# A product-key expert layer routed by column group for four token blocks at once, with sixteen best-entry tiles summed early

## The chip, the cores and the metric

The kernel runs on one core of one Trainium2 chip. The metric is the device time of one execution in microseconds; lower is better. Times from the profile count from the start of its span.

## The reference

One decoder block on 1024 tokens of width 1024: normalisation and modulation by a conditioning vector, a projection to 14 groups of 512 columns, a gated linear attention branch and a spatial gating branch, an output projection, and then a mixer with 16384 experts of one neuron each. Only the mixer is touched here. Cut to what matters:

```python
q = einsum('btd,dq->btq', h, w_q).reshape(B, T, H, 2, 128)      # H = 8 heads
s1, s2 = einsum(q[..., 0, :], keys1), einsum(q[..., 1, :], keys2) # 128 scores each
v1, i1 = top_k(s1, 16);  v2, i2 = top_k(s2, 16)
cand = v1[..., :, None] + v2[..., None, :]                        # 256 candidates
top_s, pos = top_k(cand, 16);  idx = i1 * 128 + i2 at pos
g = softmax(top_s)
y = sum over heads and 16 entries of g * gelu(h . down[idx]) * up[idx]
x = x + gate2 * y;  out = rms_norm(x, final_norm_w)
```

## The kernel before

The 1024 tokens are eight blocks of 128, in two halves of four blocks (0 to 3, 4 to 7). Each half runs through dense stages: the 14 projection groups (`group`, L1045, eight k-steps each), the output projection (`w_out_part`), the block's rows for the mixer (`h2_part`), and the query projection in four column groups of two heads each (`w_q`, L1350). A weight tile `wt` is split into two float32r parts, `wh` on ACT and `wl` on POOL or DVE (L1036, L1038), and three matmuls stand for one product (`mm3`). After every k-step `step()` advances four queues of generators by rates of their own: `qa` (conditioning rows), `qr` (routing), `qp` (the stream of expert tiles) and `qdir` (best entries of the first half). The framework then orders the instructions of each engine; in that order each engine works them off.

`s_part` (L1390) scores one column group of one block against the keys and ranks it with `tops`: the best 8 of 128 for two heads and both key halves. When all four column groups are done, `rank` (L1383) adds for each of the four blocks a `routing` (L278): 20 candidate sums per head (`cand`, L289), the best 8 of them, gates, and the decoding of their expert numbers. Of each head the best entry stays apart (`dix`, its expert; `dgt`, its gate). The other seven entries with a gate that counts go into one list per block: `pack_list` (L252) counts them (L261), gives each a place, splits the list (`th`, `tl`) and writes it to DRAM. A head of a token whose eighth gate still counts is rare: `rare` (L324) collects such heads of a group of blocks, fetches their scores (`qsc`, L362) and ranks 16 of them. The groups are blocks 0 to 3, 4 and 5, 6 and 7.

The experts' rows are worked in tiles of 128. Each tile is one gather of 128 rows of 8 KB (`uv`, L440: down and up row together) on POOL's queue, a product with the token rows on DVE, gelu and scaling on ACT, and a sum into PSUM on PE (`acc`, L513). A best-entry tile (`direct_list`, `direct_dot`, L450, L454) has one row per token, for one head of one block. A list tile (`entry_list`, `entry_dot`) reads 128 list places (`tps`, L462), spreads the token rows by matmuls (`hps`, L492, L493) and multiplies them with the gathered rows (L494). In the dense stage a list tile's sum is four float32r matmuls (`split_add`, L523, L524). A block has 8 best-entry tiles, 10 list tiles and one tile that adds the stored rows of its rare heads (`rare_rows`); then `finish` (L552) writes its output. Best entries of blocks 0 to 3 are summed apart in the dense stage (`direct_rows`) and added in `finish` through a stored row (L559).

`peer_stream` (L644) writes that order out by hand in `todo`: 6 rare tiles of group 0, blocks 0 to 3, and then for each of the two later groups:

```python
b = GROUPS[gi][0]
todo += [(b, j) for j in range(PH)] + [(NBLK + gi, PH + j) for j in range(NTR[gi])]
todo += [(b + 1, j) for j in range(PH)] + [(c, j) for c in (b, b + 1) for j in range(PH, last + 1)]
```

Here j below 8 is a best entry, up to 17 a list tile, 18 the rare rows; `NBLK + gi` stands for a group's rare tiles. `fill` (L701) starts the gathers ahead (2 tiles in the dense stage, 7 after) and holds back block 4 and what follows until the last query columns are ranked, the rest until the dense stage ends. After that, tiles have nine buffers in three pools (L1421).

## Time and profile before

| | us |
|---|---|
| runs, median of 3 | 1657.19 (1652.46 to 1660.2) |
| the profiled execution | 1650.64 |
| its span | 1648.5 |
| PE busy | 1440.4 (87%) |
| DVE busy | 1069.7 (65%) |
| POOL busy | 816.3 (50%) |
| ACT busy | 775.4 (47%) |

The span is one execution as the profiler saw it; the device time of the same execution lies 2.1 us around it. PE is TensorE, DVE VectorE, ACT ScalarE, POOL GpSimd, PEld the weight loads of TensorE. A busy share over the span is a mean over stages with different limits, so the stretches are read one by one: what an engine did in each, and what ended its waits. PEclk is the granted clock of TensorE as a share of full speed, and the DMA share is the mean busy share of the 16 DMA engines.

### The profile page before, as it was taken

To read this page: it belongs to the slowest core of one execution; us is meant where nothing else is said; L and a number is where in the kernel's file an instruction comes from. 1 tells how busy PE (TensorE), PEld (TensorE's weight loads), DVE (VectorE), ACT (ScalarE), POOL (GpSimd) and SP (SyncE) were. 2 spreads that over 40 slices of the span, in tenths; PEclk is the share of its full clock that TensorE was granted. 3 is DMA by queue.
4 is the path that set the end of the run, shared out by engine and by line. 5 is a ranking of instruction groups with operands and counts; after the bars stand their busy time and mean duration, and the time that the engine had idled before them with its cause. 6 is when DMAs were issued, how large, how long until landed. Compare 5 with 4: busy or idle time off the path is not lost. (4 is left out here: it accounts for less than half of the span.)

```text
span 1648.5 us, 20446 instructions
## 1 busy us (share of the span) xinstructions
PE 1440.4 (87%) x6113; PEld 1077.6 (65%) x6113; DVE 1069.7 (65%) x2906; ACT 775.4 (47%) x1708; POOL 816.3 (50%) x685
## 2 busy tenths in 40 slices
PE   4999989999998998888879999989879964898895
PEld 3777757888768886677657776867578842454442
DVE  6774653111454469978977777789895567678663
ACT  3553323333445355735445565566544443445442
POOL 4331247533374338755666677557775423323420
PEclk7999999999999999999999999999989976899997
DMA  9642533224376338757745787958866453998992
GB/s 306 230 165 85 188 117 109 94 79 141 109 244 247 116 116 301 247 159 243 265 163 188 249 305 275 343 213 283 304 214 210 168 233 115 365 417 310 409 403 96
DMA packets 124441, 363.81 MB, mean 221 GB/s; under 512 B 17577, under 2 KB 28073, under 8 KB 108194
## 3 DMA queue, kind: packets, MB, share of 16 engines
q0 software_dynamic: 30816, 178.14, 28.6%
q1 hardware_dynamic: 70272, 132.15, 24.1%
q10 hardware_dynamic: 23234, 52.14, 8.8%
q8 instruction: 49, 0.80, 0.2%
q14 instruction: 70, 0.57, 0.1%
HBM read 336.44 MB, written 25.94 MB: 220 GB/s over the span
## 5 line engine op out<-in xcount | busy, mean ns | idle before, releaser
L1038 POOL TENSOR_TENSOR wl<-wt,wh 128x512 fp32r<-128x512 f32 x257 | 360.6, 1409 | 368.5 <-ACT wh L1036 344.4
L1036 ACT ACTIVATE wh<-wt 128x512 fp32r<-128x512 f32 x368 | 228.0, 627 | 314.0 <-PE mm L173 177.3
L172 PE MATMUL mm<-wl,hTh 128*128 128x512 f32 x896 | 364.7, 407 | 9.7 <-POOL wl L1038 8.3
L171 PE MATMUL mm<-wh,hTh 128*128 128x512 f32 x896 | 336.4, 411 | 27.8 <-DVE sg L1239 8.8
L173 PE MATMUL mm<-wh,hTl 128*128 128x512 f32 x896 | 358.5, 403 | 1.4 <-DVE hTl L995 1.4
L171 PEld LDWEIGHTS mm<-wh,hTh 128*128 128x128 f32 x896 | 171.7, 193 | 78.1 <-DVE sg L1239 9.6
L172 PEld LDWEIGHTS mm<-wl,hTh 128*128 128x128 f32 x896 | 172.6, 193 | 59.4 <-POOL wl L1038 14.6
L1038 DVE TENSOR_TENSOR wl<-wt,wh 128x512 fp32r<-128x512 f32 x111 | 100.3, 905 | 165.8 <-ACT wh L1036 160.3
L173 PEld LDWEIGHTS mm<-wh,hTl 128*128 128x128 f32 x896 | 172.3, 192 | 41.8 <-DVE hTl L995 1.5
L171 PE MATMUL mm<-hTh,wh 128*128 128x512 f32 (+1 forms) x448 | 168.5, 378 | 10.9 <-ACT hTh L167 4.6
L440 POOL DMA_INDIRECT uv<-in_tab_dram,ix x94 | 102.0, 1085 | 147.2 <-PE hps L493 27.5
L172 PE MATMUL mm<-hTl,wh 128*128 128x512 f32 (+1 forms) x448 | 165.7, 371 | 1.0 <-DVE hTl L168 1.0
L173 PE MATMUL mm<-hTh,wl 128*128 128x512 f32 (+1 forms) x448 | 158.2, 373 | 6.6 <-POOL wl L1038 5.9
L494 DVE SCALAR_TENSOR_TENSOR uv<-uv,hps 128x512 f32<-128x512 f32 x148 | 98.3, 682 | 49.8 <-PE hps L493 26.1
L171 PEld LDWEIGHTS mm<-hTh,wh 128*128 128x128 f32 x448 | 87.7, 196 | 27.7 <-ACT vt L1083 5.9
L522 DVE SCALAR_TENSOR_TENSOR vl<-uv,r,vh 128x512 fp32r<-128x512 f32 x92 | 81.6, 915 | 36.4 <-ACT vh L521 33.7
L173 PEld LDWEIGHTS mm<-hTh,wl 128*128 128x128 f32 x448 | 86.5, 196 | 21.8 <-POOL wl L1038 6.8
L513 PE MATMUL acc<-uv,W 128*128 128x512 f32 x192 | 96.6, 628 | 3.5 <-ACT W L506 3.2
L172 PEld LDWEIGHTS mm<-hTl,wh 128*128 128x128 f32 x448 | 87.7, 196 | 14.5 <-DVE hTl L168 1.7
L492 PE MATMUL hps<-hh,E 128*128 128x512 f32 x148 | 76.3, 519 | 22.3 <-DVE uv L494 10.9
L513 PE MATMUL acc<-uv,Wd 128*128 128x512 f32 x128 | 63.4, 647 | 8.8 <-ACT Wd L454 6.9
L521 ACT ACTIVATE vh<-uv,r 128x512 fp32r<-128x512 f32 x92 | 62.2, 714 | 3.8 <-PE acc L523 1.4
(955 smaller groups left out, 2642.8 us busy)
## 6 DMA issues: line engine op xcount, KB each, us to landing
wt<-in_w_inp_dram SPq DMA_DIRECT2D x224, 256.0 KB
wt<-in_w_qp_dram SPq DMA_DIRECT2D x80, 256.0 KB
wada<-in_w_ada_dram SPq DMA_DIRECT2D x32, 512.0 KB
wt<-in_w_outp_dram SPq DMA_DIRECT2D x64, 256.0 KB
wada<-in_w_ada_dram SPq DMA_DIRECT2D x32, 256.0 KB
s_d<-so ACTq DMA_DIRECT2D x32, 256.0 KB
xr<-in_x_dram ACTq DMA_DIRECT2D x8, 512.0 KB
x_d<-x ACTq DMA_DIRECT2D x8, 512.0 KB
```

The source lines that it names most:

```text
L171: nc.tensor.matmul(ps, lh, rh, start=first, stop=False)
L172: nc.tensor.matmul(ps, lh, rl, start=False, stop=False)
L173: return nc.tensor.matmul(ps, ll, rh, start=False, stop=last).ins
L440: nc.gpsimd.indirect_dma_start(out=uv[:], out_offset=None, in_=tab, in_offset=bass.IndirectOffsetOnAxis(ap=ix, axis=0))
L492: nc.tensor.matmul(hps, Ej, hh[:, sl], start=True, stop=False)
L494: nc.vector.scalar_tensor_tensor(uv[:, sl], uv[:, sl], 1.0, hps, op0=OP.mult, op1=OP.mult, accum_out=r[:, 2 + n:3 + n])
L513: nc.tensor.matmul(acc[:, sl], W, v[:, sl], start=first, stop=last)
L521: nc.scalar.activation(vh, v, AF.Identity, scale=r[:, 5:6])
L522: nc.vector.scalar_tensor_tensor(vl, v, r[:, 5:6], vh.bitcast(F32), op0=OP.mult, op1=OP.subtract)
L1036: nc.scalar.activation(wh, wt, AF.Identity)
L1038: eng.tensor_tensor(wl, wt, wh.bitcast(F32), op=OP.subtract)
```

## The change

It routes by column group. `tops` now ranks into tables that hold one column group (two heads) of four blocks; right after a column group's scores `rank(q)` adds a `route` for it, so that the first three of four run beside the next columns' projection. The work of one `route` is as wide as that of one `routing` was: two heads of four blocks in place of eight heads of one. One `pack_half` then packs the lists of four blocks together, and one `rare` covers blocks 4 to 7, with 6 tiles in place of 4 and 4. In `todo`, after block 3, come the best-entry tiles of blocks 5 (four), 6 (four) and 7 (eight); their sums are stored by `rows_keep` and added in `finish`. Then come block 4's eight best entries, three of its list tiles, the six rare tiles, the rest of block 4, and blocks 5, 6 and 7 with what is left. `fill` lets a best-entry tile go in the dense stage as soon as its column group is ranked. Block rows have two buffers after the dense stage, and two rates change.

```diff
-GROUPS = ((0, 1, 2, 3), (4, 5), (6, 7))
+GROUPS = ((0, 1, 2, 3), (4, 5, 6, 7))
-NTR = (6, 4, 4)
+NTR = (6, 6)
-DA = 8
+EARLY = ((5, 4), (6, 4), (7, 8))
-RP3 = .5
+RP3 = .65
-RR = 0.5
+RR = 1.0
...
+    def pack_half(hf, tsel, rps):
+        n, b0 = NCS, hf * BH
+        bs = slice(b0, b0 + BH)
+        g, rk = tsel[:, :, 2 * n:3 * n], tsel[:, :, 0:n]
+        wk = rp.tile([P, 2, BH, n], F32, name="wk", tag="so", bufs=2)
+        nz, inc = wk[:, 0], wk[:, 1]
+        nc.vector.tensor_scalar(nz, g, TINY, None, op0=OP.is_ge)
+        nc.vector.tensor_tensor_scan(inc.rearrange("p b n -> p (b n)"), ones[:, 0:1].to_broadcast([P, BH * n]),
+                                     nz.rearrange("p b n -> p (b n)"), 0.0, op0=OP.mult, op1=OP.add)
+        nc.vector.tensor_copy(e4[:, 1:], inc[:, :, n - 1])
+        nc.vector.tensor_tensor(cnt[:, bs], e4[:, 1:], e4[:, :BH], op=OP.subtract)
+        yield
+        pst = rps.tile([P, BH], F32, name="aux", tag="aux")
+        nc.tensor.matmul(pst, ltri, cnt[:, bs], start=True, stop=True)
+        yield
...
+        nc.scalar.activation(th, tsel, AF.Identity)
+        nc.gpsimd.tensor_tensor(tl, tsel[:, :, n:3 * n], th[:, :, n:3 * n].bitcast(F32), op=OP.subtract)
+        nc.scalar.dma_start(tsh_d[hf][:, :, :3 * n + 2], th.bitcast(F32))
+        nc.scalar.dma_start(tsh_d[hf][:, :, 3 * n + 2:], tl.bitcast(F32))
+        routed.update(range(b0, b0 + BH))
...
+    def rows_keep(b, acc):
+        y = rowp.tile([P, D], F32, name="yd", tag="row")
+        nc.scalar.activation(y, acc, AF.Identity)
+        nc.scalar.dma_start(y_d[b], y)
+        summed.add(b)
...
+        seg(NBLK, range(PH, PH + NTR[0]))
+        for b in range(BH):
+            seg(b, range(0 if b not in summed else PH, last + 1))
+        for b, n in EARLY:
+            seg(b, range(n))
+        done = dict(EARLY)
+        seg(BH, range(last - AH), False)
+        seg(NBLK + 1, range(PH, PH + NTR[1]))
+        todo.extend((BH, j) for j in range(last - AH, last + 1))
+        closes[BH, last] = True
+        for b in range(BH + 1, NBLK):
+            seg(b, range(done.get(b, 0), last + 1))
...
-                if len(use) == 1 and b >= BH and b != NBLK and (b > BH or j >= DA or b not in topped):
+                if len(use) == 1 and b >= BH and b != NBLK and (j >= PH or (1, j // 2) not in topped):
                     break
...
+            elif lst and j < last:
+                rows_keep(b, accs[b])
...
-            for b in blks:
-                rank(b)
...
+                if half != 0:
+                    rank(q)
...
+            def rank(q):
+                tv, ti = tvi[q]
+                nc.vector.scalar_tensor_tensor(dixq[hf][q].rearrange("p b h -> p (b h)"), ti[:, :, 0, 0], float(NK),
+                                               ti[:, :, 1, 0], op0=OP.mult, op1=OP.add)
+                topped.add((hf, q))
+                qr.add(route(hf, q, tsel, tv, ti))
+                if q == 3:
+                    qr.add(pack_half(hf, tsel, aux))
+                    qr.add(rare(hf, aux))
...
-    use.append(peer_pools("1", "left", UVB, 1, 2, AH, EB, True))
+    use.append(peer_pools("1", "left", UVB, 2, 2, AH, EB, True))
```

How the order moves, at three places. First PE, at the second half's last scores (the four matmuls on `keyst`), before; `acc_12153` is block 4's sum, and the matmuls on `cnt` are packings and the rare count:

```order
L1394 MATMUL aux_12023<-keyst_95,qt_11964 128x128
L1394 MATMUL aux_12023<-keyst_95,qt_11966 128x128
L1394 MATMUL aux_12023<-keyst_95,qt_11968 128x128
L1394 MATMUL aux_12023<-keyst_95,qt_11970 128x128
L261 MATMUL aux_12169<-cnt_130,ltri_63 128x1
L513 MATMUL acc_12153<-uv_12074,Wd_12146 128x512 x2
L513 MATMUL acc_12153<-uv_12077,Wd_12151 128x512 x2
L513 MATMUL acc_12153<-uv_12080,Wd_12415 128x512 x2
L513 MATMUL acc_12153<-uv_12083,Wd_12441 128x512 x2
L513 MATMUL acc_12153<-uv_12086,Wd_12487 128x512 x2
```

Now; `acc_12111` is block 7's sum of best entries:

```order
L1462 MATMUL aux_12264<-keyst_95,qt_12206 128x128
L1462 MATMUL aux_12264<-keyst_95,qt_12208 128x128
L1462 MATMUL aux_12264<-keyst_95,qt_12210 128x128
L1462 MATMUL aux_12264<-keyst_95,qt_12212 128x128
L556 MATMUL acc_12111<-uv_12073,Wd_12109 128x512 x2
L556 MATMUL acc_12111<-uv_12104,Wd_12156 128x512 x2
L556 MATMUL acc_12111<-uv_12151,Wd_12202 128x512 x2
L556 MATMUL acc_12111<-uv_12197,Wd_12335 128x512 x2
L556 MATMUL acc_12111<-uv_12313,Wd_12368 128x512 x2
L556 MATMUL acc_12111<-uv_12316,Wd_12400 128x512 x2
L297 MATMUL aux_12440<-cnt_127,ltri_63 128x4
```

Eight of block 7's tiles follow the last scores, where one block's packing and block 4's tiles did; one packing with four columns stands for four.

Second PE, inside the last column group's projection, now (`mm` are the projection's sums, `acc_11825` block 6's best entries; before, no such sum stands there):

```order
L179 MATMUL mm_11951<-hTh_181,wh_12116 128x512
L180 MATMUL mm_11951<-hTl_182,wh_12116 128x512
L556 MATMUL acc_11825<-uv_11741,Wd_11792 128x512 x2
L181 MATMUL mm_11951<-hTh_181,wl_12117 128x512
L179 MATMUL mm_11952<-hTh_181,wh_12116 128x512
L180 MATMUL mm_11952<-hTl_182,wh_12116 128x512
L181 MATMUL mm_11952<-hTh_181,wl_12117 128x512
```

A best-entry sum stands between two matmuls of one product; blocks 5 and 6 have eight of them ahead of the last scores.

Third POOL, from the splitting of a list (`tl`) to the first rare gathers (`ix` from a list row, `dix` best entries), before:

```order
L273 TENSOR_TENSOR tl_12179<-tsel_12097,th_12178 128x112
L273 TENSOR_TENSOR tl_12253<-tsel_12184,th_12252 128x112
L289 TENSOR_TENSOR cidx_12447<-tif_12448 128x8x8
L289 TENSOR_TENSOR cidx_12447<-tif_12448 128x8x4 x3
L362 DMA qsc_12289<-s_d1_110,qix_12283 128x256
L418 DMA h2l_12377<-h2_d1_107,rtok1_137 128x1024
L289 TENSOR_TENSOR cidx_12746<-tif_12747 128x8x8
L289 TENSOR_TENSOR cidx_12746<-tif_12747 128x8x4 x3
L273 TENSOR_TENSOR tlq_12372<-qtsel_12347,thq_12371 128x32
L440 DMA uv_12407<-in_tab_dram,ix_12405 128x2048
L440 DMA uv_12429<-in_tab_dram,ix_12427 128x2048
```

Now:

```order
L311 TENSOR_TENSOR tl_12465<-tsel_9770,th_12464 128x448
L483 DMA uv_12498<-in_tab_dram,ix_12496 128x2048
L483 DMA uv_12537<-in_tab_dram,ix_12535 128x2048
L483 DMA uv_12581<-in_tab_dram,ix_12579 128x2048
L405 DMA qsc_12569<-s_d1_109,qix_12561 128x256
L461 DMA h2l_12679<-h2_d1_107,rtok1_133 128x1024
L279 TENSOR_TENSOR tlq_12674<-qtsel_12649,thq_12673 128x32
L483 DMA uv_12709<-in_tab_dram,ix_12707 128x2048
L483 DMA uv_12731<-in_tab_dram,ix_12729 128x2048
```

Before, the fetch of rare scores (`qsc`) stood between two routings and ahead of every list gather; now it stands behind three gathers of block 4's list, and no routing is left there.

## Rows read from the trace of the kernel before

**Rows 1.** Busy us (instructions) of PE, PEld, DVE, ACT, POOL; PEclk, DMA share, GB/s.

```profile
1240.00:1329.00 89.00, 89.00 (x438) 74.16 (x438) 42.52 (x189) 40.26 (x80) 42.66 (x34) 1.00 0.49 171
1329.00:1405.00 76.00, 35.34 (x106) 20.58 (x105) 60.69 (x395) 34.68 (x98) 25.94 (x39) 0.67 0.55 210
1405.00:1629.00 224.00, 200.74 (x574) 103.46 (x572) 152.06 (x587) 103.00 (x335) 69.92 (x70) 0.96 0.89 358
640.00:720.00 80.00, 64.74 (x230) 48.00 (x230) 75.77 (x207) 50.83 (x91) 57.48 (x49) 0.87 0.67 224
880.00:1240.00 360.00, 324.03 (x1469) 257.08 (x1468) 290.64 (x567) 206.87 (x472) 236.79 (x192) 0.95 0.75 266
```

**Rows 2.** The same view, one stretch of 40 us in the tail.

```profile
1560.00:1600.00 40.00, 36.38 (x113) 19.22 (x111) 24.65 (x99) 16.58 (x54) 14.42 (x15) 1.00 1.01 419
```

**Rows 3.** Waits of PE from 1331 to 1425 us: total, times, longest.

```profile
PE aux L261 <- ACT rd L452: 15.1, 1, 15.1
...
PE aux L261 <- DVE cnt L258: 11.3, 1, 11.3
```

**Rows 4.** Timeline of POOL: start us, us, instruction, idle before and its releaser.

```profile
1295.85 2.40 POOL L560 TENSOR_TENSOR fin<-fin,g2row 128x1024 f32<-128x1024 f32 x1 [8.16 <-DVE fin L559]
...
1336.16 1.02 POOL L440 DMA_INDIRECT uv<-in_tab_dram,dix  x1 [0.16 <-DVE ts L295]
...
1351.63 0.42 POOL L273 TENSOR_TENSOR tl<-tsel,th 128x112 fp32r<-128x112 f32 x1 [3.67 <-ACT th L272]
...
1369.97 0.98 POOL L362 DMA_INDIRECT qsc<-s_d,qix  x1 [1.87 <-DVE rtok L357]
...
1390.92 0.95 POOL L440 DMA_INDIRECT uv<-in_tab_dram,ix  x1 [5.32 <-PE tps L462]
...
1460.69 0.95 POOL L362 DMA_INDIRECT qsc<-s_d,qix  x1 [0.30 <-DVE jk L468]
...
1612.90 0.94 POOL L440 DMA_INDIRECT uv<-in_tab_dram,ix  x1 [7.49 <-PE hps L493]
```

**Rows 5.** Chain that ended last, from 1200 us on: start us, us, what.

```profile
1329.25 1.57 PE aux L1394 x14
...
1373.54 0.48 DVE qtv L190 x2
...
1388.74 0.62 PE tps L462 x2
...
1405.39 3.53 PE acc L513 x4
...
1426.42 10.57 PE acc L513 x24
...
1476.25 0.53 DVE qti L191 x3
...
1524.26 10.73 DMA uv<-in_tab_dram,ix
...
1604.19 0.23 PE hps L492
...
1610.41 1.72 PE acc L513 x4
...
1613.06 1.72 PE acc L513 x4
```

**Rows 6.** Waits of PE from 600 to 760 us.

```profile
PE mm L173 <- POOL wl L1038: 5.9, 3, 3.8
...
PE aux L261 <- DVE cnt L258: 1.8, 1, 1.8
```

**Rows 7.** Groups of DVE, 640 to 720 us, then 1331 to 1410: busy us, mean ns.

```profile
L289 DVE TENSOR_TENSOR cand<-tv 128x32 f32<-128x32 f32 (+1 forms) x8 | 5.1, 683 | 0.0
...
L450 DVE SCALAR_TENSOR_TENSOR uv<-uv,h2l 128x1024 f32<-128x1024 f32 x9 | 11.2, 1240 | 0.4 <-DMA uv<-in_tab_dram,dix 0.4
...
L289 DVE TENSOR_TENSOR cand<-tv 128x32 f32<-128x32 f32 (+1 forms) x16 | 2.2, 193 | 0.0
```

More of the change, by code (lines that the diff above doesn't have):

```diff
@@ L146, in block_kernel @@
     yr_d = [dram.tile([P, D], F32, name=f"yr_d{g}") for g in range(NG)]
-    y_d = dram.tile([BH, P, D], F32, name="y_d")
+    y_d = [dram.tile([P, D], F32, name=f"y_d{b}") for b in range(NBLK)]
     ncs_of = [NCS] * NBLK + [TOPK] * NG
-    ts_d = [dram.tile([P, 5 * n + 2], F32, name=f"ts_d{i}") for i, n in enumerate(ncs_of)]
+    tsh_d = [dram.tile([P, BH, 5 * NCS + 2], F32, name=f"tsh_d{i}") for i in range(NHALF)]
+    ts_d = [tsh_d[b // BH][:, b % BH] for b in range(NBLK)]
+    ts_d += [dram.tile([P, 5 * TOPK + 2], F32, name=f"ts_d{g}") for g in range(NG)]
     rt = ctx.enter_context(tc.tile_pool(name="rt", bufs=1))
@@ L157, in block_kernel, with dcol @@
     rcol = [rt.tile([P, len(bs)], F32, name=f"rcol{g}") for g, bs in enumerate(GROUPS)]
-    dix = [rt.tile([P, PH], I32, name=f"dix{b}") for b in range(NBLK)]
-    dgt = [rt.tile([P, PH], F32, name=f"dgt{b}") for b in range(NBLK)]
+    dixq = [[rt.tile([P, BH, 2], I32, name=f"dix{hf}_{q}") for q in range(4)] for hf in range(NHALF)]
+    dgtq = [[rt.tile([P, BH, 2], F32, name=f"dgt{hf}_{q}") for q in range(4)] for hf in range(NHALF)]
+    e4 = rt.tile([P, BH + 1], F32, name="e4")
+    nc.vector.memset(e4, 0.0)
+    def dcol(tabs, b, h):
+        return tabs[b // BH][h // 2][:, b % BH, h % 2:h % 2 + 1]
     def rstd_of(dst, ss, n, eng=nc.vector):
@@ L276, in pack_list @@
         routed.add(col)
-    def routing(b, tv, ti, rps):
-        gi, bi = GRP[b]
-        K1 = KS - 1
-        tsel = r2.tile([P, 3 * NCS + 2], F32, name="tsel")
-        cand = r2.tile([P, PH, NCAND], F32, name="cand")
-        cidx = r2.tile([P, PH, NCAND], F32, name="cidx")
-        tif = r2.tile([P, PH, 2, KS], F32, name="tif")
+    def pack_half(hf, tsel, rps):
[13 more added lines that the diff above has]
+        yield
+        off = r2.tile([P, BH], F32, name="off")
+        nc.vector.tensor_copy(start[:, bs], pst)
+        nc.vector.tensor_tensor(off, start[:, bs], e4[:, :BH], op=OP.subtract)
+        nc.vector.tensor_tensor(end[:, bs], start[:, bs], cnt[:, bs], op=OP.add)
+        rki = rp.tile([P, BH, n], I32, name="rki", tag="bits")
+        for i in range(BH):
+            nc.vector.tensor_scalar(rki[:, i], inc[:, i], off[:, i:i + 1], None, op0=OP.add)
+        nc.vector.tensor_scalar(rki, rki, P - 1, None, op0=OP.bitwise_and)
+        nc.vector.scalar_tensor_tensor(rk, rki, 1.0, nz, op0=OP.add, op1=OP.mult)
+        th = rp.tile([P, BH, 3 * n + 2], F32R, name="th", tag="v")
+        tl = rp.tile([P, BH, 2 * n], F32R, name="tl", tag="so", bufs=2)
+        nc.scalar.activation(th, tsel, AF.Identity)
[3 more added lines that the diff above has]
+        routed.update(range(b0, b0 + BH))
+        yield
@@ L285, in routing, with route @@
+    def route(hf, q, tsel, tv, ti):
+        K1, R = KS - 1, 2 * BH
+        if q == 0:
+            for i in range(BH):
+                nc.scalar.activation(tsel[:, i, 3 * NCS:3 * NCS + 2], lane1.to_broadcast([P, 2]), AF.Identity,
+                                     bias=lane0(hf * BH + i) - 1.0)
+        cand = r2.tile([P, R, NCAND], F32, name="cand")
+        cidx = r2.tile([P, R, NCAND], F32, name="cidx")
+        tif = r2.tile([P, R, 2, KS], F32, name="tif")
         nc.scalar.activation(tif[:, :, 0], ti[:, :, 0], AF.Identity, scale=float(NK))
@@ L377, in rare @@
         yield
-        yield from pack_list(tsel, TOPK, NBLK + gi, rps, "q")
+        yield from pack_rare(tsel, TOPK, NBLK + gi, rps, "q")
         yield
@@ L445, in direct_list @@
         r = pl["pq"].tile([P, 3], F32, name="rd", bufs=pl["ahead"] + 4)
-        return pl, b, h, h2, r, gather(ul, dix[b][:, h:h + 1])
+        return pl, b, h, h2, r, gather(ul, dcol(dixq, b, h))
     def direct_dot(ent):
@@ L778, in peer_rest @@
                 nc.vector.scalar_tensor_tensor(id_, sel[:, 0], float(NK), sel[:, 1], op0=OP.mult, op1=OP.add)
-                y = pg_.tile([P, D], F32, name="gy")
+                y = pl["ph"].tile([P, D], F32, name="gy", tag="hh")
                 nc.vector.memset(y, 0.0)
```

126 lines of the change are left out of this document (59 added, 67 removed).

## The prediction

> **What bounds the kernel now.** I read the stretches by engine first, then the waits, then the chain that ended last. The stretches [rows 1] show three regimes. While the last query columns of the second half are projected (1240 to 1329) TensorE is busy 89.00 of 89.00 us: whatever is put on it there costs its own length. From 1329 to 1405 it is busy 35.34 of 76 us and the DMA engines 0.55: here the scores are ready and the lists are not. From 1405 to 1629 it is busy 200.74 of 224 us with the DMA at 0.89 and 358 GB/s: the tail of gathered tiles. In a 40 us piece of that tail the DMA share is 1.01 at 419 GB/s [rows 2]; a gather brings 128 rows of 8 KB, 1.05 MB, so at that rate one costs 2.51 us, and at the tail's mean of 358 GB/s 2.93 us.
>
> The middle regime is what the change is about. TensorE's two longest waits there stand both before a list packing's count: 15.1 us, released when a best-entry tile was scaled, and 11.3 us for the counts themselves [rows 3]. The queue of gathers [rows 4] shows it from the other side: block 4's eight best-entry gathers go out from 1336.16 on, one after the other, and the next gather goes only at 1390.92, because in this order four rare tiles come next, and they need the routing of blocks 4 and 5 and the rare chain. Of 80 gathers behind the last scores (the last goes at 1612.90) only 8 are issued in the first 60 us.
>
> **What a tile costs in the tail.** On the chain [rows 5] list tiles at the end follow each other every 2.65 us (1610.41, 1613.06), 1.72 of it the four sums; six best-entry tiles take 10.57 us (x24), 1.76 each. With 2.51 us of DMA, gather and TensorE are nearly level for a list tile, and the DMA is the longer for a best-entry tile.
>
> **The change, part by part.** The clock below starts at the last scores (1329.25, first of rows 5), S.
>
> *Tiles taken out of the tail.* Before, the first rare tile is summed at 1405.39 [rows 5], S+76, with 8 best-entry tiles done and 76 tiles to go (48 list or rare, 24 best-entry, 4 of stored rare rows). After, the orders put 19 gathered tiles ahead of the first rare one: 8 of block 7, 8 of block 4, 3 lists of block 4. Behind it stand 43 list or rare tiles, 8 best-entry, 4 stored: 5 and 16 fewer. They are cheapest by TensorE, 5 x 2.65 + 16 x 1.76 = 41.4 us; by the DMA at its full rate 21 x 2.51 = 52.7; at the tail's mean rate 21 x 2.93 = 61.5. I take **57 us**, between the last two: the DMA is the nearest bound, and the tail never held its full rate throughout. Two rare tiles fewer and one rare chain fewer are in this count; so is the second buffer for a block's rows (hb 2), which I give nothing of its own.
>
> *The dense stage.* Eight early tiles (blocks 5 and 6) stand between the last projections in TensorE's order, 8 x 1.76 = +14 us where it is full. Against that the orders put four list tiles fewer among the last five hundred projection matmuls, since the first half's routing is done sooner and the stream of tiles starts sooner; such a tile has eight matmuls of the 0.23 us that the chain shows for one (1604.19 [rows 5]), so 4 x 1.8 = -7, into 880 to 1240, where TensorE idles 36 of 360 us [rows 1]. In the first half three of four routings move from 640 to 720, where VectorE is busy 75.77 of 80 us and TensorE idles 15.3 [rows 1], to the projections before. Bounds nothing and 15; I take -5, as the waits that name the routing are small (the counts, 1.8 us in 600 to 760 [rows 6]). Sum **+2**, bounds -9 and +14. Eight more products of 1.24 us [rows 7] and three routings go on VectorE beside these projections. A routing is at most 12 us: the 60.69 us of VectorE from 1329 to 1405 [rows 1] hold four and nine products. That is at most 47 us where 46.5 of the 89 are free, and four list tiles are gone: hidden, just. If that cover went, the rival on the dense stage below applies. Seven early gathers share the DMA with the weights at a share of 0.49.
>
> *The chain to the lists.* Before, block 4's list is split at 1351.63 [rows 4], S+22.4, with three products in between. After, VectorE's order has eight products ahead of the packing's end, 5 x 1.24 = +6.2, and one packing for four blocks, on 224 columns in place of 56: +2. Split at S+31. Six more products, 7.4, stand ahead of the first list row, then 5 (an estimate: 2.2 us from a list row at 1388.74 to its gather at 1390.92 [rows 4, 5], as much again for the last product's scaling and sum): first list gather at S+43. The list's way through DRAM runs beside these products, in two writes on ACT's queue where four blocks had eight. POOL's order has three list gathers and then the fetch of the rare scores, each about 1.25 us apart: S+48. That fetch took 3.6 us with an empty queue (1369.97 to 1373.54) and up to 15.6 behind gathers (1460.69 to the ranking of these scores at 1476.25) [rows 4, 5]. Three 1.05 MB gathers are ahead of it: I take 10, S+58. From there to the first rare gather before: 1373.54 to 1390.92, 17.4, S+75; to its sum 14.5 before, beside three routings on VectorE, which are gone: 7. The first rare sum comes at S+82 against S+76: **+6**, bounds -6 and +20. What is late next is the same queue: between the last of the 19 tiles and the rare ones the DMA still idles, some 20 us.
>
> *The end.* Block 7 now adds a stored sum: its last chain goes through a POOL product of 2.40 us [rows 4] that it did not have. **+3**. Three more rows of 512 KB written and read cost 3 x 1.3 us of DMA, inside the 57.
>
> **Sum.** The profiled execution took 1650.64 us: -57 + 2 + 6 + 3 = -46, 1604.6. The median of the runs shown, 1657.19, lies 6.6 above that execution; against it the forecast is **1611 us**. Bounds of the four terms against the median: 1657 - 61.5 - 9 - 6 + 3 = 1584 and 1657 - 41.4 + 14 + 20 + 3 = 1653.
>
> **Rivals.**
>
> *More is saved.* The tail's bubbles (two waits of over 10 us for a gather, one of them 10.73 us [rows 5]) lie where blocks and rare groups change; with one group and two row buffers they go, the dense end does not move, and the rare fetch finds an empty queue: 1584. For it: one group change instead of two. Against: the six rare tiles still wait for everything.
>
> *VectorE and POOL stand in each other's way in the dense stage.* The four sums of candidates of a routing took 193 ns each in the tail and 683 ns between 640 and 720, where POOL splits weights [rows 7], and TensorE waited 5.9 us for POOL's splits in 600 to 760 [rows 6]. The change moves three routings and eight products beside POOL's splits of the last columns, all of which are on POOL there. At the loss of 640 to 720 (15.3 of 80 us) the 89 us lose 17: 1628. For: those rows. Against: 640 to 720 also had the recurrent heads, and POOL is at 42.66 of 89 us here, not at 57 of 80. The Trainium skill (SBUF — State Buffer, "SBUF: two separate sides") says that VectorE instructions with two SBUF inputs and GpSimd instructions that read SBUF take one pair of ports as an exclusive lock, the loser waiting for the whole instruction. By that rule every candidate sum and product put there would wait for a split, and a split for it; the 683 against 193 ns agree, and the rule would give this rival's time rather than mine if the splits had no slack.
>
> *The one packing comes late.* All lists now hang on the last column group, on one packing and one rare chain; if the rare scores take 15.6 us and the chain slows as it did beside routing, the first rare sum comes at S+102, 20 later than taken: 1631. For: VectorE's order puts two list products ahead of the rare ranking. Against: 19 tiles are served meanwhile.
>
> *Slower.* TensorE takes its instructions in order, and the eight early sums stand at fixed places between projections. Each waits for its gather, its product and a scaled identity; if they are late, projections wait behind them. The price is eight times that lateness. From 5.8 us each the 46 us are eaten, from 6.8 us each the kernel is slower by over 0.5%; at the 10.73 us above, 1611 + 86 = 1697. Against: in 1240 to 1329 TensorE idled not at all, although list tiles stand in the same way between the same matmuls.
>
> That the change doesn't do what it says is settled by the orders: eight early tiles do stand ahead of the last scores, and eight (block 7) only behind them, and so they are priced.
>
> **How the numbers follow.** 0.5% is about what a measurement of this kernel can tell from no change. Forecast (1596 to 1626) 0.57; more is saved 0.12; the dense stage 0.14; late packing 0.11; slower 0.06. The two middle rivals together, 1648 and more, come to about 0.05 out of theirs. Faster by over 0.5% 0.88, within 0.5% 0.05, slower 0.07. The range runs from 1580, a little past the larger saving, to 1642, past each middle rival alone.
>
> **What would show it.** Right: between the last scores and the first rare sum TensorE sums 19 tiles instead of 8 and its share there rises well above 35 of 76 us; the last scores start within 10 us of 1329; the first rare sum follows them by about 82; the last stretch is about 50 us shorter at an unchanged rate. Wrong: waits for gathers or products ahead of early sums inside the projections; POOL's splits named by TensorE's waits after 1240; a rare fetch that lands later than S+65; a last stretch that shrinks by 41 or less, TensorE being its bound.

## The result, and the profile after

| | us |
|---|---|
| after, median of 4 runs | 1636.44 (1634.42 to 1637.92) |
| before, median of 4 runs | 1658.38 (1652.46 to 1660.2) |
| ratio, with 95% interval | 0.9876 (0.9854 to 0.9898) |
| the profiled execution after, its span | 1637.25, 1635.2 |

The change saves 22 us by the medians, where 46 were forecast. The time lies inside the range, at its slow end. The kernel before had medians of 1651.7 to 1658.4 in the sessions that follow, so kernels of different sessions are compared by their ratios to it.

Three points cut the profiled execution: the last row of scores on PE, the first rare sum, the end. The timeline of PE, before and then after (start us, us, instruction, idle before and its releaser):

```profile
1331.50 2.05 PE L1394 MATMUL aux<-keyst,qt 128*128 128x128 f32 x16 [0.46 <-ACT so L1396]
```

```profile
1312.38 1.22 PE L1462 MATMUL aux<-keyst,qt 128*128 128x128 f32 x4 [6.03 <-ACT qt L1415]
...
1355.35 3.68 PE L556 MATMUL acc<-uv,Wd 128*128 128x512 f32 x4 [2.43 <-ACT yd L689]
1358.86 1.95 PE L1462 MATMUL aux<-keyst,qt 128*128 128x128 f32 x16
...
1396.24 10.57 PE L556 MATMUL acc<-uv,Wd 128*128 128x512 f32 x24 [0.84 <-ACT Wd L497]
1406.24 0.64 PE L505 MATMUL tps<-thl,E 128*128 128x170 f32 x1
```

The first rare sum stands in the chain that ended last, after (start us, us, what):

```profile
1356.87 13.38 DMA s_d<-so
...
1412.89 8.16 DMA qsc<-s_d,qix
...
1433.97 1.81 DMA thl<-ts_d
...
1449.84 3.78 PE acc L556 x4
```

Before, it stood at 1405.39 [rows 5]. So, from profiled execution to profiled execution (1650.64 to 1637.25, -13.4; these two happen to lie nearer each other than the medians):

| stretch | before | after | difference | forecast |
|---|---|---|---|---|
| to the last row of scores | 1331.5 | 1358.9 | +27.4 | +2 |
| from there to the first rare sum | 73.9 | 91.0 | +17.1 | +6 |
| from there to the end of the execution | 245.2 | 187.4 | -57.8 | -57 + 3 |

The tail gave what was forecast. The expected gain was given back ahead of it, most of it before the last scores. A second execution of the changed kernel (after_again, below) has its last row of scores at 1353.8, +22.3: it reached the last columns 5 us earlier, so about 5 of the 27.4 differ from execution to execution. The same stretches by engine, after (busy us and instructions of PE, PEld, DVE, ACT, POOL; PEclk, DMA share, GB/s), answering to [rows 1]:

```profile
1240.00:1359.00 119.00, 110.35 (x487) 84.55 (x486) 79.44 (x344) 62.01 (x131) 62.16 (x59) 0.96 0.72 249
1359.00:1450.00 91.00, 57.40 (x147) 29.30 (x145) 59.23 (x304) 38.12 (x110) 28.56 (x30) 0.74 0.66 249
1450.00:1613.00 163.00, 148.88 (x448) 81.14 (x448) 108.15 (x393) 73.42 (x240) 47.92 (x47) 0.96 0.89 359
```

The last row is the tail at an unchanged rate (DMA 0.89, 359 GB/s against 0.89, 358), 61 us shorter. In the first row PE, which had been busy 89.00 of 89.00, idles 8.65 of 119. The middle row has 18 tiles where 19 were forecast, because block 7's first sum went ahead of the last row of scores (1355.35). PE is busy 57 us instead of 35, but it is 15 us longer than the one it answers to, and the DMA share is still only 0.66.

### The profile page after: what moved, and what is told of

Read it like the earlier page. It is cut to its first block, busy times and chain, and to the rows that moved or that the text cites. A ratio compares the mean times of both kernels' runs of the same rounds, so it can differ in the third digit from the quotient of the medians.

```text
span 1635.2 us, 20174 instructions
## 1 busy us (share of the span) xinstructions
PE 1428.3 (87%) x6076; PEld 1073.5 (66%) x6076; DVE 1074.3 (66%) x2766; ACT 772.5 (47%) x1682; POOL 821.9 (50%) x677
## 4 chain that ended last, share of the span: by engine, by line
PE 40%; DVE 23%; DMA 15%; issue 9%; ACT 7%; POOL 5%; ACTq 0%; DVEq 0%; POOLq 0%; SPq 0%
PE mm L180 8%; PE mm L179 8%; PE mm L181 8%; PE acc L556 7%; DMA uv<-in_tab_dram,ix 3%; DMA wada<-in_w_ada_dram 2%; POOL wl L1098 2%; DVE wl L1098 2%; DMA uv<-in_tab_dram,dix 2%; DMA uvd<-in_down_dram,dix 2%; DVE uv L537 2%; DVE vl L565 1%; PE hps L535 1%; DVE E L634 1%; DVE uvd L670 1%
## 5 line engine op out<-in xcount | busy, mean ns | idle before, releaser
L1098 POOL TENSOR_TENSOR wl<-wt,wh 128x512 fp32r<-128x512 f32 x257 | 368.6, 1440 | 379.7 <-ACT wh L1096 342.2
L565 DVE SCALAR_TENSOR_TENSOR vl<-uv,r,vh 128x512 fp32r<-128x512 f32 x92 | 91.3, 1023 | 29.7 <-ACT vh L564 28.1
L556 PE MATMUL acc<-uv,W 128*128 128x512 f32 x184 | 91.9, 625 | 3.4 <-ACT W L549 2.1
L556 PE MATMUL acc<-uv,Wd 128*128 128x512 f32 x128 | 67.5, 668 | 22.6 <-ACT Wd L497 18.7
```

The costliest lines, as they stand in the source:

```text
L556: nc.tensor.matmul(acc[:, sl], W, v[:, sl], start=first, stop=last)
L565: nc.vector.scalar_tensor_tensor(vl, v, r[:, 5:6], vh.bitcast(F32), op0=OP.mult, op1=OP.subtract)
L1098: eng.tensor_tensor(wl, wt, wh.bitcast(F32), op=OP.subtract)
```

## Experiments

Where an experiment leaves a part of the kernel out, its output is not the kernel's; it serves only to price that part. For the dense stage one stretch serves all kernels: from the second score row of the first column group (1259.40 after) to the last row of scores (1358.86), which holds the projections of the other three groups. After, and in the kernel without early tiles (hold_all, below), it holds the same 232 recorded projection matmuls.

| kernel | ratio to before (95%) | stretch, us |
|---|---|---|
| after | 0.9876 (0.9854 to 0.9898) | 99.5 |
| after_again | 0.9869 (0.9841 to 0.9897) | 99.5 |
| hold_67 | 0.9833 (0.9782 to 0.9884) | 91.3 |
| no56 | 0.9811 (0.9762 to 0.9861) | 78.9 |
| hold_all | 0.9766 (0.9716 to 0.9815) | 73.3 |
| hold_all_again | 0.9735 (0.9710 to 0.9759) | 74.0 |
| dropsum | 0.9833 (0.9788 to 0.9878) | 93.1 |
| dropscale | 0.9861 (0.9824 to 0.9897) | 89.8 |
| dropprod | 0.9801 (0.9758 to 0.9844) | 80.1 |
| nofin3 | 0.9824 (0.9805 to 0.9843) | 94.1 |
| dropsum_nofin3 | 0.9797 (0.9771 to 0.9823) | 88.6 |
| tsel_dve | 0.9848 (0.9803 to 0.9894) | 97.3 |
| hold_tsel_dve | 0.9744 (0.9704 to 0.9783) | 72.2 |

**No early tile before the dense stage ends (hold_all).**

```diff
-                if len(use) == 1 and b >= BH and b != NBLK and (j >= PH or (1, j // 2) not in topped):
+                if len(use) == 1 and b >= BH and b != NBLK:
```

> The changed kernel, but no best-entry tile of blocks 4 to 7 may start before the dense stage has ended; the list of tiles is the same, so 24 best-entry tiles and 3 list tiles now stand between the last scores and the first rare sum. Theory (the eight to nine early sums on TensorE's in-order queue are what pushed the dense end back: 16 us of their own, 8.5 us of waits, and score copies held behind their scalings on ScalarE): the last scores start at 1330 to 1335 again instead of 1358.9, the first rare sum comes at 1420 to 1430 instead of 1449.8, and the time falls by 20 to 28 us against the changed kernel, to 1608 to 1617. Rival A (the routing beside the projections is what pushed the end back): the last scores stay past 1350 and the time is that of the changed kernel or worse. Rival B (what bounds the time up to the first rare sum is the traffic of the gathers, not the chain of packing and rare scores): the last scores go back to 1332, but eight more gathers behind them push the first rare sum out again, past 1440, and less than 10 us are saved.

Measured: last row of scores at 1326.47, first rare sum at 1420.97, median 1613.73; in the repeat, beside the changed kernel in one session, 1613.14 against 1635.57. That is 22 us faster than the changed kernel, and 2.3 to 2.7% faster than the kernel before: with those of its variants below that change nothing, it is the fastest version found. The theory holds, rivals A and B do not: the traffic is heavier behind the scores (24 best-entry and 3 list tiles, DMA share 0.80 over those 94 us), yet the first rare sum comes 29 us earlier. By stretches:

```profile
1240.00:1327.00 87.00, 84.79 (x416) 69.87 (x415) 60.40 (x302) 43.78 (x85) 49.19 (x50) 1.00 0.67 229
1327.00:1421.00 94.00, 69.64 (x178) 34.29 (x176) 72.39 (x333) 48.05 (x143) 32.88 (x34) 0.84 0.80 312
1421.00:1586.00 165.00, 151.35 (x452) 81.97 (x450) 108.02 (x396) 72.90 (x241) 50.90 (x50) 0.95 0.90 362
```

One detail matters: the edit moves products, scalings and sums behind the last scores, but not all gathers. The framework still issues nine of them on POOL's queue between 1260.72 and 1326.24, and they cost the stage nothing that can be seen: TensorE is busy 71.06 of the 73.26 us. Two of the nine go out only in the last 1.5 us of the stretch, so this is shown for seven. Behind the stage it is not shown to be free: the chain that ended last there holds a write of score copies of 8.59 us (1326.94) and a load of token rows of 8.65 us (1336.55), and no run tells whether the gathers lengthen these.

> The changed kernel once more, unaltered, beside the next one on the same chip and with five rounds: its ratio to the kernel before should lie within 0.985 to 0.990 again (0.9876 before).

> The kernel without early tiles in the dense stage once more, unaltered, beside the changed kernel on the same chip. Theory: 15 to 25 us below the changed kernel, and below the kernel before by 2.2 to 2.9%. If the gap is under 8 us, the first comparison (on two chips) misled.

Both as expected (0.9869 and 0.9735).

**A half dose, and fewer tiles behind the scores (hold_67, no56).** hold_67, and what no56 has beside hold_all's edit:

```diff
-                if len(use) == 1 and b >= BH and b != NBLK and (j >= PH or (1, j // 2) not in topped):
+                if len(use) == 1 and b >= BH and b != NBLK and (b > 5 or j >= PH or (1, j // 2) not in topped):
```

```diff
-EARLY = ((5, 4), (6, 4), (7, 8))
+EARLY = ((7, 8),)
```

> As the changed kernel, but only block 5's four best-entry tiles may start in the dense stage; those of 6 and 7 wait for its end. A dose between none and eight. Theory: each early sum costs the dense end about 3 us, so the last scores start near 1343 (half way), and the time lies half way between the changed kernel and the one with none, near 1624. Rival (a fixed cost, one wait at one place, whatever the number): the last scores start where all eight had them (1356 or later) or where none had them.

> No tile of blocks 4 to 7 in the dense stage, and only block 7's eight best entries ahead of block 4's; those of blocks 5 and 6 stay in their places behind the rare tiles. 16 best-entry and 3 list tiles between the last scores and the first rare sum: what the prediction counted, without its early tiles. Theory: last scores at 1330 to 1335, first rare sum at 1412 to 1420, but eight more tiles behind it at 2.5 to 2.9 us: 8 to 18 us less than the changed kernel (1618 to 1628), and 5 to 12 more than with all 16 behind the scores. Rival B (traffic): the first rare sum comes 20 us earlier than with all sixteen, and the two take the same time.

The half dose gives a time half way (0.9833), but the stretch does not lie half way: four early tiles cost it 18 us, the other five 8. So the price per tile is not one number; waits of one place are in it. TensorE idles 10.4 us of the stretch with four early tiles (7.7 of it for copies of the query columns, `qt`) and 8.7 with nine, against 2.2 without: both doses pay about the same wait, and the last five add the length of their sums. no56 ends later than hold_all by 8 us although its first rare sum comes 2 us earlier (1419.01): from there on its eight more tiles cost 201.4 - 189.7 = 11.7 us, 1.5 each, less than either price that the prediction weighed. It has no early tile in the stage and still one wait of 5.0 us for `qt`, to which the section on `qt` comes back.

**The parts of six early tiles left out one by one (dropsum, dropscale, dropprod).**

```diff
-                add_rows(wv, accs[b], fst, lst)
+                if (b, 4) in EARLY and j < 4:
+                    fst = lst
+                if lst or not ((b, 4) in EARLY and j < 4):
+                    add_rows(wv, accs[b], fst, lst)
```

dropscale adds this in `direct_dot`, and dropprod the same two lines ahead of the product:

```diff
         nc.vector.scalar_tensor_tensor(uv[:, :D], uv[:, :D], 1.0, h2, op0=OP.mult, op1=OP.mult, accum_out=r[:, 0:1])
+        if (b, 4) in EARLY and h < 3:
+            return 0, 0
```

> The changed kernel, and of the four early best-entry tiles of blocks 5 and 6 only the last is summed (the other three of each, six in all, are gathered, multiplied and scaled as before, but their sums into PSUM are left out of the computation). It parts the sums' own length on TensorE (six of 1.88 us) from what the tiles' gathers, products and scalings cost the dense stage elsewhere. Theory (mostly the length: TensorE is full there, so a sum costs what it takes): the last scores start 10 to 14 us earlier than in the changed kernel (1345 to 1349 against 1358.9) and the time falls by 9 to 14 us, to 1622 to 1627. Rival (the length is hidden in the waits; the gathers and products are the cost): the last scores move by less than 5 us.

> The changed kernel, and of the same six early tiles of blocks 5 and 6 the gelu, the scalings on ScalarE and the sums are left out of the computation; gathers and products stay. Theory (ScalarE works in order, and each scaling waits for its product, so copies of the dense stage stand behind gathers): the last scores start 5 us or more before those of the run without the sums alone (1354), and the ratio to the kernel before is 0.978 to 0.981 (0.9833 there). Rival (ScalarE has slack): the ratio stays at 0.982 to 0.985.

> As before it, with the products of these six tiles on VectorE left out of the computation too: only their gathers stay. Theory (VectorE's products of 1.2 us have room): within 4 us of the run with products. Rival (products beside splits and routing are the cost): 6 us or more below it, a ratio of 0.975 or less. If the gathers alone are the cost, the ratio stays at 0.982 or more in both.

Of six sums, 11.3 us long, the stretch got back 6.4: TensorE's wait for `qt` grew from 6.0 to 12.5 us instead. Leaving the scalings out too gave 3.3 more, leaving the products out 9.7 more. The gains expected of the first two were too high; in the third the rival is right, though not to its full 0.975. In this order of leaving out, the products give the most. Another order could share the 19.4 us out otherwise, since each omission moves the waits: dropscale has one of 6.9 us for `rd`, the scaling's column, which the changed kernel has not. The time of dropscale (0.9861) missed both its theory and its rival, and does not follow its stretch; in that execution the stage reached the stretch 7 us later than after (1266.01 against 1259.40), which these omissions do not explain, so I judge it by the stretch alone. Waits in the stretch show why products weigh so much (engine, line, what for: us in total, times, longest); DVE after, then ACT after, then DVE in hold_all:

```profile
DVE uv L493 <- DMA uv<-in_tab_dram,dix: 10.4, 5, 3.5
DVE tv L192 <- ACT so L1464: 4.2, 4, 1.4
...
DVE uv L493 <- PE mm L181: 2.6, 2, 1.4
...
DVE uv L493 <- issue: 2.1, 1, 2.1
```

```profile
ACT rd L494 <- DVE uv L493: 15.1, 8, 5.1
ACT tsel L364 <- DVE v L362: 7.9, 3, 3.2
...
ACT dd L205 <- DVE dd L204: 4.0, 1, 4.0
```

```profile
DVE tv L192 <- ACT so L1464: 11.0, 6, 4.0
DVE vl L565 <- ACT vh L564: 6.5, 2, 3.9
DVE v L358 <- ACT v L341: 3.1, 1, 3.1
```

VectorE takes its instructions in order and stood still 15.1 us in front of early products (L493), 10.4 of it until their gathers landed; the rankings and routings behind them stood still too. ScalarE stood 15.1 us in front of the scalings (L494) that need these products, and the copies of the query columns (`qt`) and scores (`so`) behind those. TensorE then waits for the copies. One link of this, from ScalarE after: the last matmuls of a row of scores began at 1288.38 and took 1.50 us, but their copy ran only here, behind a scaling that waited for its product:

```profile
1294.10 0.20 ACT L494 ACTIVATE rd<-rd 128x1 f32<-128x1 f32 x1 [5.08 <-DVE uv L493]
1294.21 0.58 ACT L1464 ACTIVATE so<-aux 128x512 f32<-128x512 f32 x1
```

With nothing early, VectorE still waits, 20.6 us in the three groups shown, but only for the stage's own work. So it is not the waiting alone that costs, but what waits behind it.

**The wait of 6.0 us for `qt` (nofin3, dropsum_nofin3, tsel_dve, hold_tsel_dve).** What stood ahead of `qt` on ACT, after:

```profile
1306.48 0.26 ACT L205 ACTIVATE dd<-dd 128x64 f32<-128x64 f32 x1 [4.02 <-DVE dd L204]
...
1310.50 0.30 ACT L364 ACTIVATE tsel<-v 128x56 f32<-128x56 f32 x1 [3.25 <-DVE v L362]
1310.70 1.04 ACT L608 ACTIVATE fin<-fin 128x1024 f32<-128x1024 f32 x1
...
1311.74 0.58 ACT L1415 ACTIVATE qt<-mm 128x512 f32<-128x512 f32 x1
```

Two steps of a routing that wait for VectorE, and block 3's norm. nofin3 leaves out what follows the first sum of block 3's finish, on POOL and on ScalarE; dropsum_nofin3 leaves out that and dropsum's six sums; tsel_dve moves a copy:

```diff
             nc.vector.tensor_tensor(y, y, acc, op=OP.add)
+            if b == 3:
+                nc.sync.dma_start(out[0, b * P:(b + 1) * P, :], y)
+                return
```

```diff
-        nc.scalar.activation(tsel[:, :, c0:c0 + 2 * K1], w[:, :, 0].rearrange("p (b k) -> p b k", b=BH), AF.Identity)
+        nc.vector.tensor_copy(tsel[:, :, c0:c0 + 2 * K1], w[:, :, 0].rearrange("p (b k) -> p b k", b=BH))
```

> The changed kernel, and of block 3's finish in the dense stage only the sum with the stored rows is kept; its multiplications, its addition, its norm (three operations of 2.4 us on POOL, two of 1 us on ScalarE) are left out of the computation. In the changed kernel they run at 1299.9 to 1306.4, where the routing of the second half's second column group has one sum of candidates of 2.59 us, and TensorE waits 6.0 us for a copy (qt) behind both on ScalarE. Theory (this wait is VectorE and POOL in each other's way, and a part of the slip of its own): the wait falls under 2 us, the last scores start 4 to 8 us earlier, and the time falls by 4 to 8 us. Rival (the routing makes ScalarE late by itself): the wait stays above 4 us and the time within 3 us.

> Both of the last omissions together: six of the eight early sums of blocks 5 and 6, and block 3's finish but for its first sum, left out of the computation. In the run with the sums alone left out the wait for the copy grew from 6.0 to 12.5 us, so that of 11 us only 6.6 came back. Theory (length of the sums, and this wait, are the two parts of the slip, and each hides some of the other): the last scores start at 1338 to 1345 against 1358.9, and the time falls by 14 to 20 us. Rival (the parts do not add, something else holds the dense end): under 10 us.

> The changed kernel with one edit that computes the same: the routing's last copy (56 columns of tsel) is made on VectorE, where its input comes from, and not on ScalarE. In the changed kernel it stands ahead of the copies qt on ScalarE and waits 3.25 us for VectorE. Theory (the query copies are held by the routing's steps on ScalarE): TensorE's wait of 6.0 us for qt falls to 3 us or less, the last scores start 3 to 6 us earlier, and the ratio is 0.983 to 0.985 against 0.987. Rival (the wait moves to the next instruction, the norm of block 3 or the exponentials): the ratio stays within 0.985 to 0.989.

> The same edit on the kernel without early tiles, where TensorE waits 0.9 us for qt: nothing to gain at that place. Theory: within 5 us of that kernel (ratio 0.9735 to 0.9766 in two sessions). Rival (ScalarE's queue also holds up the chain behind the last scores): 6 us or more below it.

Without block 3's finish the wait falls to 1.7 us, the stretch by 5.4, the time by about 7 us (0.9824 against 0.9869 in the same session): as its theory said. But nofin3 takes away POOL's operations and two steps of the norm on ScalarE (1.04 and 1.15 us) together, the first of them directly ahead of `qt`, so it does not tell which of the two counted. And its stretch of 94.1 us, with TensorE busy 91.0, is still some 20 us above the one without early tiles. Both omissions together save 12 us, between the two expectations: a wait of 8.1 us for `qt` has come back, again behind a routing step on ScalarE. The copy moved to VectorE takes the wait to 2.7 us and the stretch 2.2 down; the time (0.9848) is in the expected place, but its interval takes in the changed kernel. Without early tiles the same edit does nothing, as expected.

Something else than early work is in this wait. In every kernel here in which TensorE waits 5 us or more for `qt`, the routing's copy `tsel` (L364) stands ahead of `qt` on ScalarE; in hold_all it comes after. no56, then hold_all, neither with an early tile:

```profile
1305.03 0.29 ACT L364 ACTIVATE tsel<-v 128x56 f32<-128x56 f32 x1 [4.50 <-DVE dgt L352]
1305.23 1.55 ACT L1415 ACTIVATE qt<-mm 128x512 f32<-128x512 f32 x3
```

```profile
1297.72 1.55 ACT L1415 ACTIVATE qt<-mm 128x512 f32<-128x512 f32 x3
...
1307.95 0.30 ACT L364 ACTIVATE tsel<-v 128x56 f32<-128x56 f32 x1 [3.41 <-DVE tv L192]
```

With the same 354 recorded instructions of TensorE, no56's stretch is 5.6 us longer. So up to some 5 of the 25.9 us between the changed kernel and hold_all hang on which copy the framework put first, and not on the early tiles' own work. No run has `qt` first with early tiles in place, so this stays open.

That VectorE is late there seems to have a second cause, read from rows and not tested by itself. VectorE's sums of candidates after, then in hold_all, then one subtraction and POOL's rows at the same moment in dropsum:

```profile
1299.71 2.59 DVE L330 TENSOR_TENSOR cand<-tv 128x32 f32<-128x32 f32 x3
```

```profile
1294.80 0.57 DVE L330 TENSOR_TENSOR cand<-tv 128x64 f32<-128x64 f32 x4
```

```profile
1303.73 4.01 DVE L204 TENSOR_TENSOR dd<-ts 128x64 f32<-128x64 f32 x1
```

```profile
1304.09 2.35 POOL L606 TENSOR_TENSOR fin<-fin 128x1024 f32<-128x1024 f32 x1
1306.38 1.26 POOL L1101 TENSOR_TENSOR wl<-wt,wh 128x512 fp32r<-128x512 f32 x1
```

The subtraction took 0.20 us in the third column group's routing of the changed kernel (1339.87). Here it began 0.36 us before POOL's first operation and ended at 1307.74, when both had ended (1307.64). The Trainium skill (SBUF — State Buffer, "SBUF: two separate sides") describes a pair of ports that VectorE, with two inputs in SBUF, and GpSimd, reading SBUF, take as an exclusive lock, for a whole instruction. The rows agree, and show one small instruction that lasts as long as two of POOL's in a row.

**The routing beside the projections (late1, late1_forced, late0_forced)**, on hold_all. Routings are added only when the fourth column group is ranked (late1 and late1_forced in the second half, late0_forced in the first); the forced ones also tie their sums of candidates on VectorE, and of candidate numbers on POOL, behind the half's last ranking. For this the rankings have four buffers instead of two, and late0_forced keeps one constant in another pool:

```diff
-                qr.add(route(hf, q, tsel, tv, ti))
+                late_q = hf in LATEQ
+                for c in (range(4) if q == 3 else ()) if late_q else (q,):
+                    qr.add(route(hf, c, tsel, *tvi[c]))
...
+        with tc.issue_after(last_ix[0]) if hf in LATEQ else ExitStack():
```

> The kernel without early tiles in the dense stage, and in the second half the first three column groups are routed only after the last scores, together with the fourth, as the kernel before did (there by block). This measures what the routing beside the projections is worth by itself. Theory (three routings of about 10 us on VectorE are hidden beside the projections): packing, first list gather and first rare sum come 20 to 30 us later, the last scores at most 4 us earlier, and the time is 15 to 28 us above the kernel without early tiles. Rival A (they stand in the way of the splits there, and the dense end pays for them): the last scores start 10 us or more earlier and the time is about the same.

> As late1, but in late1 the framework put the three routings back to where their inputs are ready, so that its order was that of the kernel without early tiles; here their candidate sums are tied behind the last ranking on VectorE. Theory: three routings of about 10 us on VectorE come to stand behind the last scores, so the packing's count comes 15 to 30 us later than without early tiles (1364.3), and the time is 10 to 25 us above that kernel (1613.7). Rival A (in the dense stage they cost what they save): the last scores start 3 us or more earlier, the packing comes at the same time and so does the end.

> The kernel without early tiles, and in the first half the four column groups are routed only after the half's last scores, tied there on VectorE, as the kernel before did. The prediction gave the earlier routing 5 us in the half's boundary and 7 us from list tiles that move forward. Theory (neither reached the end: at the 148th and at the 348th of 368 weight splits the changed kernel stood 5 us behind and level): the time is within 6 us of the kernel without early tiles (1613.7). Rival (they are worth the 12 us and were eaten by something else): 8 us or more above it.

late1 (1608.8, 0.9731) told nothing: its candidate sums ran at 1259.9, 1295.0, 1317.2 and 1349.0, as in hold_all, since the framework orders by readiness. Forced, the second half pays 22 us (1635.83, 0.9881): the packing's count comes at 1374.9 instead of 1364.3, 10.6 us later where 15 to 30 were expected, and the first list gather at 1416.4 instead of 1394.9, while the stretch gets only 2.3 us shorter (71.0). So routing by column group beside the projections is worth its place. In the first half it is worth nothing: 1613.73 (0.9748), last row of scores at 1329.1.

**The rare fetch ahead of gathers (qfirst)**, on hold_all: block 4's best-entry gathers are queued behind `qsc`, and the routing is run on until `qsc` has been issued.

```diff
+                with tc.issue_after(qsc_ins[1]) if b == BH else ExitStack():
...
+    while 1 not in qsc_ins:
+        qr.pump()
```

> The kernel without early tiles, and on POOL's queue the eight gathers of block 4's best entries are tied behind the fetch of the rare scores, which took from 1371.6 to about 1396 behind eight gathers. Theory (from the last scores to the first rare sum a chain through DRAM sets the time, and its fetch waits behind gathers): the rare fetch lands in 6 to 12 us, the first rare gather goes 10 to 18 us earlier than 1412, and the time falls by 4 to 12 us against 1613.7. Rival (from the last scores on the gathers' traffic sets the time, the DMA share being 0.8 and more): the first rare gather goes earlier, but the time stays within 4 us, or is worse because the DMA idles before the fetch.

From the fetch's issue to the ranking of its scores it took 3.3 us (1376.15 to 1379.48) instead of 11.5 (1371.62 to 1383.11; the expectation's "to about 1396" was a misreading). The 11.5 are not the fetch's alone: the ranking stood on VectorE behind two products that waited for their gathers. But the fetch went out 4.5 us later, the first rare gather not earlier than before (1416.9 for 1412.1), and the time is not better (1621.36, 0.9777). Neither the theory nor the rival said this of the rare gather; the edit does not pay, and whether the tiles' traffic or the chain is the bound there it does not decide.

## Why the prediction was right and wrong

**The tail: right in sum.** -57 and +3 were forecast, -57.8 measured, at the forecast rate. Its make-up is less sure. In no56, one execution against another, a best-entry tile costs 1.5 us in the tail, below the 1.76 and 2.51 that were weighed; 16 of these and 5 list tiles of 2.65 make 37 us, and the other 20 would then be bubbles of the second rare group, which the rival "more is saved" named. In that case the sum came out by luck: tiles priced too dear, bubbles put at nothing. That group was not taken out by itself, so this split stays open.

**The dense stage: this step failed.** The sum +2 was 14 for eight early sums, less 12 for work done sooner, with the products and routings "hidden, just", that is at nothing. Measured: +27.4, in the second execution +22.3. All three parts were off. Without early tiles the last row of scores stands 2 to 7 us before that of the kernel before (1324.3 to 1329.2, in two executions of it and one with the moved copy, against 1331.5), so of the 12 a part came; the first half's routing, priced at 5, gave none. With early tiles the stretch is 25.9 us longer (99.5 against 73.3 and 74.0). On TensorE nine sums stand ahead of the last row, not eight, and are busy 18.7 us; its idle time grows by 6.4 us, from 2.20 to 8.65. After and without early tiles:

```profile
1259.40:1358.86 99.46, 90.81 (x390) 68.17 (x389) 68.72 (x319) 51.85 (x107) 48.23 (x47) 0.95 0.73 251
```

```profile
1253.21:1326.47 73.26, 71.06 (x354) 58.58 (x352) 52.21 (x283) 37.21 (x71) 39.56 (x42) 1.00 0.67 233
```

The 8.65 are 6.03 for `qt`, 2.43 for `yd`, the copy of block 6's sum out of PSUM, and 0.2 besides. The granted clock is 0.95 after and 1.00 without. Right behind the 6.03 us without work it was 0.50, the lower level, 1.2 GHz, until 1317.3, and the sum behind the wait of 2.43 us took 3.68 us, others 1.88. The reason that fails is the one on the cover. VectorE does have the free time (68.72 busy of 99.46), but not when the products need it: they wait in order for gathers, and what the dense stage needs from VectorE and ScalarE stands behind them. The omissions show that TensorE's sums and this second path are nearly level: taking away one alone uncovers the other. As said of `qt`, some of the second path is order and not early work.

**The chain to the first rare sum: direction right, size off** (+17 for +6, from the last row of scores). Three of its steps were off. First, the last two score copies stood behind scalings on ScalarE, and the very last also behind the write of an earlier copy, whose buffer it takes (issued at 1356.87, 13.38 us on the chain):

```profile
1367.61 0.58 ACT L1464 ACTIVATE so<-aux 128x512 f32<-128x512 f32 x1
1370.27 0.60 ACT L1464 ACTIVATE so<-aux 128x512 f32<-128x512 f32 x1 [2.08 <-DMA s_d<-so]
```

That is 11.4 us behind the last row of scores, where it was 4.2 before (1335.73). Second, the list's way was not hidden: the lists were split at 1391.82, 33.0 us behind that row where the forecast comes to 28.8, but the first list row on PE (1406.24) stands behind six best-entry sums in order (10.57 us from 1396.24), so POOL waits, after:

```profile
1391.82 1.14 POOL L311 TENSOR_TENSOR tl<-tsel,th 128x448 fp32r<-128x448 f32 x1 [3.23 <-ACT th L310]
1409.13 0.96 POOL L483 DMA_INDIRECT uv<-in_tab_dram,ix  x1 [16.18 <-ACT ix L514]
...
1412.89 0.95 POOL L405 DMA_INDIRECT qsc<-s_d,qix  x1 [0.30 <-issue]
```

Third, from the rare gather (1437.93) to its sum it took 11.9 us where 7 were given. The rare fetch, priced at 10 us, took 8.16: about right.

**The rivals.** The one that ended slower was near in kind, not in place or price: it had TensorE wait at the early sums for gathers, products or identities. It waited there for none of these, only 2.4 us for `yd`; the waits came at the projection's copies, because VectorE and ScalarE work in order too. Beyond their own length the nine sums cost 6.4 us, 0.7 each, not 5.8. The rival of VectorE and POOL was priced at 17 us. Without block 3's finish the time falls by about 7, and not all of that need be this rival; what POOL's splits cost beside VectorE no run takes out by itself. The late packing came about half as late as priced (the first rare sum 11 us behind its forecast, of 20). "More is saved" did not happen in sum.

**Slips in its working**, none of which moves the forecast: 14 early gathers were issued ahead of the last row of scores, not seven, and the DMA share was 0.73 there; by the rows used for it, four routings and nine products in 60.69 us, a routing is 12.4 us and not at most 12; the dense stage's parts add up to -8 at the least, not -9; and the candidate sums of 193 ns are from 1331 to 1410, which lies ahead of the tail.

What stays open: the make-up of the tail's 57.8 us, how much of the wait for `qt` is the order of two copies on ScalarE, and how nofin3's gain divides between POOL's operations and the norm's steps on ScalarE.

## What to carry to other kernels

Free time of an engine is cover only for work whose inputs are there: an instruction that waits for a transfer, put into the in-order queue of an engine that a full stage needs, holds up everything behind it on that engine and on those that wait for it. Move the transfer early, if its buffer is free, and leave the arithmetic on it behind the stage: here the gathers alone cost the stage nothing that can be seen, and the same tiles summed behind the last scores gave 22 us more. When a part is left out to price it, look for the wait that takes its place before believing the difference.

## What was not expected of the hardware

A subtraction of 128x64 that took 0.20 us on VectorE in another routing took 4.01 us beside two operations of POOL, 2.35 and 1.26 us: it outlasted both. Seven gathers of 1.05 MB issued beside the last projections, and two more at their end (DMA share 0.67 over the stretch), did not visibly slow these, TensorE being busy 71.06 of 73.26 us at a granted clock of 1.00.
